# S5 parameter tables beside an MLP: a new order of kp products, masked copies, sums, weight casts and low parts

## The chip, the cores and the metric

The kernel runs on one NeuronCore of one Trainium2 chip. The metric is the device time of one execution in microseconds (us). Engines: PE (TensorE, matrix products), DVE (VectorE), ACT (ScalarE), POOL (GpSimd), and SP, whose queue issues the DMAs. Each runs its own instructions in order and waits for the others by semaphores.

## The reference

One inference step of a two-layer decoder, for 512 prompt tokens and 32 sample tokens (8 sequences of 4), with the same weights. Layer 0 mixes tokens by gated linear attention, layer 1 by an S5 state-space layer; an MLP with squared ReLU follows each:

```python
def _rmsnorm(x, g): ...
for i in range(DEPTH):                       # DEPTH = 2, D_MODEL = 1024, D_FF = 4096
    h = _rmsnorm(x, prm['g_pre_mix'][i])
    m = _gla_mixer(h, ...) if i % 2 == 0 else _s5_mixer(h, ...)
    x = x + _rmsnorm(m, prm['g_post_mix'][i])
    h = _rmsnorm(x, prm['g_pre_mlp'][i])
    f = jnp.square(jax.nn.relu(h @ prm['w_up'][i])) @ prm['w_down'][i]
    x = x + _rmsnorm(f, prm['g_post_mlp'][i])
```

The S5 layer has 64 groups of 64 complex states. Its parameters need much preparation that depends on no token: the step `dt`, the eigenvalues `lam = exp(a * dt)`, `z = (lam - 1) / a`, `bb = z * b`, and products with `c`. The kernel turns the recurrence into products with tables, which it computes from these.

## The kernel before, in words

Activations lie transposed in SBUF: `X[128, 8, 544]`, features on partitions, 544 tokens in two halves of 288 and 256 columns. Products run as fp32r in three passes: high parts of weight and input (`wh`, `xh`), and the two cross terms with the low parts (`wl`, `xl`). Weights come as tiles `raw` of 128 x 1024 by DMA; `split_w` makes `wh` by a cast on ACT (line 111) and `wl = raw - wh` on POOL (line 115; at other times partly or wholly on DVE, line 113), in two parts of 128 x 512 each.

A **job** (`job`) is one weight tile times one half: 24 matmuls into one PSUM bank. Its order in code: the weight splits that a planner (`plan`) set for this job number (`split_at`), then the matmuls, then `finish`, which emits the job's evacuation (`evac`), what was deferred to this job (`after`), and one entry of the list `bg`, the background work. An entry of `bg` is called a slot here; its instructions follow the job's evacuation on every engine. A tile of a four-tile block is used by the first half's four jobs and again by the second half's, and a ring of five buffers decides how early the next cast can be.

In the MLP, "up" jobs compute `h @ w_up`: their evacuation is `r = max(ps, 0) * rs` on DVE (line 350), Square and the cast `hh` on ACT (lines 352, 353), then `hl = r - hh` on DVE (line 354). "Down" jobs multiply `hh`, `hl` with `w_down` and add the result into `acc` on DVE (line 362). Up and down alternate in blocks of 16 jobs.

During the first layer's MLP, after its first up block, `s5_prepare` fills `bg`: 21 slots of small setup work, then sixteen **units** u of four slots each, then three more slots. A unit makes the tables of four S5 groups and stores them to DRAM:

- first slot: `unit_w2` (two products `tmp` on POOL, two products `w` on DVE, lines 1008 to 1011), `unit_t` (five angle instructions `tm`, `ta` on DVE, lines 1069 to 1071)
- second: `unit_w3` (two sums `w` on DVE, lines 1016, 1017, and the store `wd<-w`), `unit_t2` (angle reduction on DVE, lines 1077 to 1080, 872), `unit_w(u+1)` (loads `zb`, `bt`)
- third: `unit_q0` (two products `tmp` on POOL, lines 1029, 1030), `unit_s` (sine `cs<-ta` on ACT, line 1085, then the angle of the cosine on DVE, lines 876 to 878)
- fourth: `unit_k(u-1)`: the kp product on PE (line 1052, eight plain fp32 matmuls of `bbd` and `q`), its copy `kk` on ACT (line 1055), two sums on DVE (line 1058), stores `md<-kk`; then `unit_q(u)`: four instructions `q` on DVE (lines 1035 to 1038), the store, four masked copies `bbd` on ACT (line 1044); then `unit_c` (cosine on ACT, line 1089, and the store)

The bank of kp is called `kp` or `held` in the profile. Of the sixteen units' slots 32 stand behind up jobs, eight at each of the four positions.

Of the kernel before, what the change touches and what calls it, by code (L numbers as in the profile page):

```python
# [12 lines left out]
AF = mybir.ActivationFunctionType  # L13
# [29 lines left out]
def f32(ap):  # L43
    return ap.bitcast(F32)
# [28 lines left out]
class Builder:  # L73
    def __init__(self, tc, io):
        self.tc, self.nc, self.io = tc, tc.nc, io
        self.jobs = 0
        self.after = defaultdict(list)
        self.before_evac = defaultdict(list)
        self.hold, self.held = set(), []
        self.n_tiles = io["w"].shape[0]  # L80
        self.raw, self.wh, self.wl = {}, {}, {}
        self.tile0 = 0
        self.plan()
        self.dve_ks = 1
        self.bg = []
        self.dve_win = None
        self.part = {}
# [5 lines left out]
            self.nc.sync.dma_start(r, self.io["w"][t].rearrange("p (k m) -> p k m", k=KD))  # L93
            self.raw[t] = r

    def split_w(self, t, part=None):

        if part is None:
            self.split_w(t, 0)
            self.split_w(t, 1)  # L100
            return
        nc = self.nc
        r = self.raw[t]
        if part == 0:
            pool = self.p_x if self.in_x[t] else self.p_w
            self.wh[t] = pool.tile([128, KD, 128], F32R, tag="wh", name="wh")
            self.wl[t] = pool.tile([128, KD, 128], F32R, tag="wl", name="wl")
        h, l = self.wh[t], self.wl[t]
        d = self.dve_ks if self.dve_win is None else self.dve_win
        a, b, c = part * 4, part * 4 + d, part * 4 + 4  # L110
        nc.scalar.activation(h[:, a:c], r[:, a:c], AF.Copy)  # L111
        if b > a:
            nc.vector.tensor_sub(l[:, a:b], r[:, a:b], f32(h[:, a:b]))  # L113
        if c > b:
            nc.gpsimd.tensor_sub(l[:, b:c], r[:, b:c], f32(h[:, b:c]))  # L115
        if part:
            del self.raw[t]
            self.load_raw(t + RAW)
# [88 lines left out]

    def finish(self, ps, evac):
        j = self.jobs
        if j in self.hold:  # L210
            self.held.append((ps, evac))
        else:
            for f in self.before_evac.pop(j, []):
                f()
            for p, e in self.held:
                e(p)
            self.held.clear()
            evac(ps)
        for f in self.after.pop(j, []):
            f()  # L220
        if self.bg:
            for f in self.bg.pop(0):
                f()
        self.jobs += 1

    def defer(self, n, f):
# [114 lines left out]
    def mlp(self, g_post, g_next, sink=None, after_first=None, before_last=None):  # L341
        nc = self.nc
        hh = self.p_p.tile([128, KD, NT], F32R, tag="Hh", name="hh")
        hl = self.p_p.tile([128, KD, NT], F32R, tag="Hl", name="hl")

        def up(m, hf, ps):
            c0, c1 = HALF[hf]
            n = c1 - c0
            r = self.p_t.tile([128, 288], F32, tag="r", name="r", bufs=3)
            nc.vector.scalar_tensor_tensor(r[:, :n], ps, 0.0, self.rs[hf][:, :n], op0=OP.max, op1=OP.mult)  # L350
            h = hh[:, m, c0:c1]
            nc.scalar.activation(r[:, :n], r[:, :n], AF.Square)  # L352
            nc.scalar.activation(h, r[:, :n], AF.Copy)
            self.defer(0, lambda: nc.vector.tensor_sub(hl[:, m, c0:c1], r[:, :n], f32(h)))  # L354

        def down(b, m, hf, ps):
            c0, c1 = HALF[hf]
            a = self.acc[:, m, c0:c1]
            if b == 0:
                nc.scalar.activation(a, ps, AF.Copy)  # L360
            else:
                nc.vector.tensor_add(a, ps, a)
            if b == 3:
                self.m_done(m, hf, g_post, g_next, sink)

        for b in range(4):
            for part in ("up", "down"):
                if part == "down" and b == 3 and before_last:
                    before_last()
                sizes = (8,) if PLAN[self.block][0] == 8 else (4, 4)  # L370
                q = 0
                for n in sizes:
                    if part == "up":
                        self.run_block(self.xh, self.xl, lambda i, hf, ps: up(q + i, hf, ps))
                    else:
                        self.run_block(hh, hl, lambda i, hf, ps: down(b, q + i, hf, ps))
                    q += n
                if part == "up" and b == 0 and after_first:
                    after_first()
# [426 lines left out]
    def s5_prepare(self, ctx):  # L806

        nc, io = self.nc, self.io
# [142 lines left out]
        st = {}  # L951
# [50 lines left out]
        def unit_w2(u):  # L1002
            w = p.tile([128, 2, 2, 2, 64], F32, tag="w", name="w")
            zb = st["zb"].rearrange("p r q (g n) -> p r q g n", g=2)
            b = [st["bt"][:, r, :, None, :].to_broadcast([128, 2, 2, 64]) for r in (0, 1)]
            zr, zi = zb[:, 0], zb[:, 1]
            tp = [tmp[:, 256 * i:256 * (i + 1)].rearrange("p (q g n) -> p q g n", q=2, g=2) for i in (0, 1)]
            G.tensor_mul(tp[0], zi, b[1])
            G.tensor_mul(tp[1], zi, b[0])
            V.tensor_mul(w[:, 0], zr, b[0])  # L1010
            V.tensor_mul(w[:, 1], zr, b[1])
            st["w"], st["tp"] = w, tp
# [14 lines left out]
        def unit_q0(u):  # L1027
            l, c, tp = q_parts(u)
            G.tensor_mul(tp[0], l[1], c[1])
            G.tensor_mul(tp[1], l[1], c[0])  # L1030

        def unit_q(u):
            q5 = p.tile([128, 2, 2, 10, 16], F32, tag="q", name="q5")
            l, c, tp = q_parts(u)
            V.tensor_mul(q5[:, 0], l[0], c[0])
            V.tensor_mul(q5[:, 1], l[0], c[1])
            V.tensor_add(q5[:, 0], q5[:, 0], tp[0])
            V.tensor_sub(q5[:, 1], q5[:, 1], tp[1])
            nc.sync.dma_start(self.qd[u].rearrange("p (a b) -> p a b", a=4),
                              q5.rearrange("p r q t c -> p (r q) (t c)")[:, :, 0:128])  # L1040
            bbd = p.tile([128, 2, 2, 2, 16], F32, tag="bbd", name="bbd")
            for r in (0, 1):
                for g in (0, 1):
                    nc.scalar.activation(bbd[:, r, :, g], self.bb[:, r, 2 * u:2 * u + 2], AF.Copy, scale=gm[:, g:g + 1])
            st["q5"], st["bbd"] = q5, bbd

        def unit_k(u):
            ps = self.bank("kp")
            q5, bbd = st["q5"], st["bbd"]
            for q in (0, 1):  # L1050
                for r in (0, 1):
                    nc.tensor.matmul(ps[0:32, q * 128:(q + 1) * 128], bbd[:, r, q].rearrange("p g c -> p (g c)"),
                                     q5[:, r, q, 2:10].rearrange("p t c -> p (t c)"), start=(r == 0), stop=(r == 1))
            kk = self.kk[0]
            nc.scalar.activation(kk[:, :, 0:128], ps[0:32, 0:256].rearrange("p (q n) -> p q n", q=2), AF.Copy)
            for q in (0, 1):
                o = kk[:, q, 96:128]
                V.scalar_tensor_tensor(o, eye, dsk[:, 2 * u + q:2 * u + q + 1], o, op0=OP.mult, op1=OP.add)
                nc.sync.dma_start(self.md[2 * u + q], kk[:, q])
# [4 lines left out]
        def unit_t(u):  # L1064

            a, m = (p.tile([128, 2, 128], F32, tag=n, name=n) for n in ("ta", "tm"))
            col = lambda n, q: t(n)[:, 2 * u + q:2 * u + q + 1]
            for q in (0, 1):
                V.tensor_scalar(m[:, q], iota, col("ptu", q), MAGIC, op0=OP.mult, op1=OP.add)
                V.tensor_scalar(a[:, q], iota, col("phi", q), None, op0=OP.mult)  # L1070
            V.tensor_scalar(m, m, MAGIC, None, op0=OP.subtract)
            st["a"], st["m"] = a, m
# [20 lines left out]
        todo = [load, rest, step_size, magnitude, angles, lams, zs, turn_angle, masks, bbar, z_rows,  # L1093
                *[rest] * 7, z_turn, rest, lambda: unit_w(0)]
        for u in range(16):
            todo += [[lambda u=u: unit_w2(u), lambda u=u: unit_t(u)],
                     [lambda u=u: unit_w3(u), lambda u=u: unit_t2(u)] + ([lambda u=u: unit_w(u + 1)] if u < 15 else []),
                     [lambda u=u: unit_q0(u), lambda u=u: unit_s(u)],
                     ([lambda u=u: unit_k(u - 1)] if u else []) + [lambda u=u: unit_q(u), lambda u=u: unit_c(u)]]
        todo += [rest, rest, lambda: unit_k(15)]  # L1100
        self.bg += [f if isinstance(f, list) else [f] for f in todo]

    def s5(self, ctx):
# [418 lines left out]
```

## Time and profile before

| what | value |
|---|---|
| median of 3 runs | 1404.31 us (1402.98 to 1405.43) |
| the profiled execution's own time | 1405.15 us |
| its span, first to last instruction | 1403.4 us |
| mean granted TensorE clock | 0.968 |
| busy: PE, DVE, ACT, POOL | 94%, 62%, 40%, 46% of the span |

Profile rows give the start in us from the span's start, the duration in us, the engine, the source line, the operation, `out<-in` by the program's names, shapes and a count; in brackets stands the idle time of the engine just before and what ended it. Rows of waits give: who waited, at which line, for which engine and line, then the sum in us, how many times, the longest. Busy times of PE come from modelled ends of pipelined matmuls. A merged row (count over 1) gives the time from the first start to the last end.

### The profile page before, as it was taken

The page shows a single profiled execution, that of the slowest core. Times are in us where ns is not written, and L with a number is a line of the kernel's source. Part 1 is how long each engine was busy: PE and PEld are TensorE (multiplying, and loading weights), DVE is VectorE, ACT ScalarE, POOL GpSimd, SP SyncE. Part 2 cuts the span into 40 slices and gives each one's busy share as a digit, 9 for nine tenths or more (in the row PEclk, how much of TensorE's full clock was granted, in tenths as well). Part 3 has the DMA queues.
Part 4 walks back from the last instruction along what each step waited for, and adds up shares of the span by engine and source line. Part 5 has one row for each costly group of instructions (what it writes and reads, how often), then busy time and mean ns, then how long its engine had stood idle before and what let it go on. Part 6 is the DMA issues. An engine that isn't in the chain of part 4 may idle for free. (4 is left out here: it accounts for less than half of the span.)

```text
span 1403.4 us, 25744 instructions
## 1 busy us (share of the span) xinstructions
PE 1312.2 (94%) x9968; PEld 1278.3 (91%) x9968; DVE 874.9 (62%) x1793; ACT 563.5 (40%) x1283; POOL 639.5 (46%) x715
## 2 busy tenths in 40 slices
PE   7999999989999898889898997899899999999996
PEld 6999999979999797789897997899799999999996
DVE  7865655597437997799648789655871342332345
ACT  6534354645333423323443332344452432432432
POOL 4443344565474674466445343443643333333240
PEclk9999999999999899999999999999999999999998
DMA  5233222312333454445332768432223232323221
GB/s 184 95 120 124 76 95 64 121 61 77 109 109 113 134 162 132 130 141 175 117 106 72 239 183 254 132 99 91 85 66 91 73 109 69 98 76 106 76 61 64
DMA packets 79274, 157.53 MB, mean 112 GB/s; under 512 B 8144, under 2 KB 41808, under 8 KB 78128
## 3 DMA queue, kind: packets, MB, share of 16 engines
q1 hardware_dynamic: 79152, 155.89, 35.6%
q8 instruction: 78, 1.28, 0.4%
q14 instruction: 44, 0.36, 0.1%
HBM read 130.27 MB, written 25.59 MB: 111 GB/s over the span
## 5 line engine op out<-in xcount | busy, mean ns | idle before, releaser
L115 POOL TENSOR_TENSOR wl<-raw,wh 128x384 fp32r<-128x384 f32 (+2 forms) x351 | 422.4, 1217 | 483.9 <-ACT wh L111 482.1
L111 ACT ACTIVATE wh<-raw 128x512 fp32r<-128x512 f32 x368 | 216.3, 618 | 86.5 <-PE held L186 53.4
L186 PE MATMUL held<-xh,wh 128*128 128x288 f32 (+1 forms) x784 | 233.0, 297 | 2.9 <-ACT wh L111 2.8
L186 PE MATMUL held<-xh,wl 128*128 128x288 f32 (+1 forms) x784 | 229.7, 293 | 3.8 <-POOL wl L115 3.8
L186 PE MATMUL held<-xl,wh 128*128 128x288 f32 (+1 forms) x784 | 230.1, 294 | 0.8 <-DVE xl L279 0.8
L186 PE MATMUL mm<-xh,wh 128*128 128x256 f32 (+1 forms) x752 | 221.8, 295 | 0.8 <-ACT wh L111 0.8
L186 PE MATMUL mm<-xl,wh 128*128 128x256 f32 (+1 forms) x752 | 220.1, 293 | 2.1 <-DVE xl L279 2.0
L186 PE MATMUL mm<-xh,wl 128*128 128x256 f32 (+1 forms) x752 | 218.5, 290 | 0.9 <-POOL wl L115 0.9
L113 DVE TENSOR_TENSOR wl<-raw,wh 128x128 fp32r<-128x128 f32 (+2 forms) x247 | 138.2, 568 | 105.6 <-ACT wh L111 100.2
L186 PEld LDWEIGHTS held<-xh,wl 128*128 128x128 f32 x784 | 150.3, 192 | 5.1 <-POOL wl L115 5.1
L186 PEld LDWEIGHTS held<-xh,wh 128*128 128x128 f32 x784 | 150.8, 192 | 4.6 <-ACT wh L111 3.0
L186 PE MATMUL held<-hh,wh 128*128 128x288 f32 (+1 forms) x512 | 150.4, 294 | 4.0 <-ACT wh L111 4.0
L186 PE MATMUL held<-hh,wl 128*128 128x288 f32 (+1 forms) x512 | 150.2, 293 | 3.1 <-POOL wl L115 3.1
L186 PEld LDWEIGHTS held<-xl,wh 128*128 128x128 f32 x784 | 150.7, 192 | 1.4 <-DVE xl L279 1.0
L352 ACT ACTIVATE r<-r 128x256 f32<-128x256 f32 (+1 forms) x128 | 55.1, 431 | 238.3 <-DVE r L350 238.3
L186 PE MATMUL mm<-hh,wh 128*128 128x256 f32 (+1 forms) x512 | 148.8, 291 | 1.7 <-ACT wh L111 1.7
L186 PE MATMUL held<-hl,wh 128*128 128x288 f32 (+1 forms) x512 | 150.0, 293 | 0.0
L186 PE MATMUL mm<-hh,wl 128*128 128x256 f32 (+1 forms) x512 | 148.2, 290 | 1.8 <-POOL wl L115 1.8
L186 PE MATMUL mm<-hl,wh 128*128 128x256 f32 (+1 forms) x512 | 148.8, 291 | 0.0
L186 PEld LDWEIGHTS mm<-xl,wh 128*128 128x128 f32 x752 | 144.8, 193 | 3.4 <-DVE xl L279 3.2
L186 PEld LDWEIGHTS mm<-xh,wh 128*128 128x128 f32 x752 | 145.1, 193 | 2.7 <-issue 1.2
L186 PEld LDWEIGHTS mm<-xh,wl 128*128 128x128 f32 x752 | 144.1, 192 | 1.1 <-POOL wl L115 1.1
(400 smaller groups left out, 2876.1 us busy)
## 6 DMA issues: line engine op xcount, KB each, us to landing
raw<-in_w SPq DMA_DIRECT2D x184, 512.0 KB
S<-in_h SPq DMA_DIRECT2D x4, 1024.0 KB
out_gla_s<-S SPq DMA_DIRECT2D x4, 1024.0 KB
zb<-zd SPq DMA_DIRECT2D x16, 256.0 KB
wd<-w SPq DMA_DIRECT2D x16, 256.0 KB
qd<-q SPq DMA_DIRECT2D x16, 256.0 KB
wd<-cs SPq DMA_DIRECT2D x16, 256.0 KB
qt<-qd SPq DMA_DIRECT2D x16, 256.0 KB
```

The costliest lines, as they stand in the source:

```text
L111: nc.scalar.activation(h[:, a:c], r[:, a:c], AF.Copy)
L113: nc.vector.tensor_sub(l[:, a:b], r[:, a:b], f32(h[:, a:b]))
L115: nc.gpsimd.tensor_sub(l[:, b:c], r[:, b:c], f32(h[:, b:c]))
L186: self.nc.tensor.matmul(ps[:, :c1 - c0], a[:, k], b[:, k, c0:c1], start=(k == 0 and i == 0), stop=(k == KD - 1 and i == 2))
L352: nc.scalar.activation(r[:, :n], r[:, :n], AF.Square)
```

## The change

Nothing is added to the computation or taken from it; the instructions are the same, in another order.

- `finish` emits the casts `wh` of the next job's splits ahead of this job's evacuation while `bg` is not empty. The subtractions stay where they were.
- `hl` of an up job goes to a list `late`, emitted behind the slot's background work. Where there is no such work its place is the old one.
- The masked copies `bbd` of unit u move to the first slot of unit u+1 (`unit_b`), kp to its second slot (`unit_k`), the copy `kk` to the third (`unit_k1`), the sums and stores to the fourth (`unit_k2`). Before, `bbd` stood in the fourth slot of unit u and the other three together in the fourth of unit u+1. The list is one slot longer.

```diff
 def split_w(self, t, part=None, cast_only=False):
...
-        nc.scalar.activation(h[:, a:c], r[:, a:c], AF.Copy)
+        if (t, part) not in self.is_cast:
+            nc.scalar.activation(h[:, a:c], r[:, a:c], AF.Copy)
+        if cast_only:
+            self.is_cast.add((t, part))
+            return
...
 def finish(self, ps, evac):
         j = self.jobs
+        if self.bg:
+            for u in self.split_at.get(self.wjob, []):
+                self.split_w(*u, cast_only=True)
...
         if self.bg:
             for f in self.bg.pop(0):
                 f()
+        for f in self.late:
+            f()
+        self.late.clear()
...
-            self.defer(0, lambda: nc.vector.tensor_sub(hl[:, m, c0:c1], r[:, :n], f32(h)))
+            self.late.append(lambda: nc.vector.tensor_sub(hl[:, m, c0:c1], r[:, :n], f32(h)))
...
+        def unit_b(u):
             bbd = p.tile([128, 2, 2, 2, 16], F32, tag="bbd", name="bbd")
...
+        def unit_k1(u):
+            nc.scalar.activation(self.kk[0][:, :, 0:128], st["kp"][0:32, 0:256].rearrange("p (q n) -> p q n", q=2), AF.Copy)
+
+        def unit_k2(u):
             kk = self.kk[0]
-            nc.scalar.activation(kk[:, :, 0:128], ps[0:32, 0:256].rearrange("p (q n) -> p q n", q=2), AF.Copy)
...
         for u in range(16):
-            todo += [[lambda u=u: unit_w2(u), lambda u=u: unit_t(u)],
-                     [lambda u=u: unit_w3(u), lambda u=u: unit_t2(u)] + ([lambda u=u: unit_w(u + 1)] if u < 15 else []),
-                     [lambda u=u: unit_q0(u), lambda u=u: unit_s(u)],
-                     ([lambda u=u: unit_k(u - 1)] if u else []) + [lambda u=u: unit_q(u), lambda u=u: unit_c(u)]]
-        todo += [rest, rest, lambda: unit_k(15)]
+            todo += [[lambda u=u: unit_w2(u), lambda u=u: unit_t(u)] + ([lambda u=u: unit_b(u - 1)] if u else []),
+                     [lambda u=u: unit_w3(u), lambda u=u: unit_t2(u)] + ([lambda u=u: unit_w(u + 1)] if u < 15 else []) +
+                     ([lambda u=u: unit_k(u - 1)] if u else []),
+                     [lambda u=u: unit_q0(u), lambda u=u: unit_s(u)] + ([lambda u=u: unit_k1(u - 1)] if u else []),
+                     ([lambda u=u: unit_k2(u - 1)] if u else []) + [lambda u=u: unit_q(u), lambda u=u: unit_c(u)]]
+        todo += [[lambda: unit_b(15)], lambda: unit_k(15), lambda: unit_k1(15), lambda: unit_k2(15)]
```

The new lines shift the numbers: `r` is line 361, `hl` 365, `q` 1046 to 1049, `bbd` 1058, kp 1066, `kk` 1071, the sums 1077, the sine 1104, L876 to L878 become 887 to 889.

The first place is DVE, the second slot of unit 1, in an up block. Before:

```order
L350 SCALAR_TENSOR_TENSOR r<-mm,rs_84 128x288
L354 TENSOR_TENSOR hl<-r,hh 128x288
L1016 TENSOR_TENSOR w<-w,tmp 128x256
L1017 TENSOR_TENSOR w<-w,tmp 128x256
L1077 SCALAR_TENSOR_TENSOR ta<-tm,ta 128x256
L1078 SCALAR_TENSOR_TENSOR ta<-tm,ta 128x256
L1080 SCALAR_TENSOR_TENSOR ta<-iota,sm,ta 128x128 x2
L872 TENSOR_SCALAR ta<-ta 128x256
```

The same place on DVE after the change:

```order
L361 SCALAR_TENSOR_TENSOR r<-mm,rs_84 128x288
L1027 TENSOR_TENSOR w<-w,tmp 128x256
L1028 TENSOR_TENSOR w<-w,tmp 128x256
L1096 SCALAR_TENSOR_TENSOR ta<-tm,ta 128x256
L1097 SCALAR_TENSOR_TENSOR ta<-tm,ta 128x256
L1099 SCALAR_TENSOR_TENSOR ta<-iota,sm,ta 128x128 x2
L883 TENSOR_SCALAR ta<-ta 128x256
L365 TENSOR_TENSOR hl<-r,hh 128x288
```

`hl` moved from directly behind `r` to the end of the slot.

The second place is ACT, the fourth slot of unit 15 and the slot behind it (`r` is here the Square, `cs` the cosine). Before:

```order
L352 ACTIVATE r<-r 128x256
L353 ACTIVATE hh<-r 128x256
L1055 ACTIVATE kk_4000<-held 32x2x128
L1044 ACTIVATE bbd<-bb,gm 128x2x16 x4
L1089 ACTIVATE cs<-ta 128x256
L111 ACTIVATE wh<-raw 128x512
L352 ACTIVATE r<-r 128x256
L353 ACTIVATE hh<-r 128x256
L111 ACTIVATE wh<-raw 128x512 x2
```

The same place on ACT after the change:

```order
L113 ACTIVATE wh<-raw 128x512
L363 ACTIVATE r<-r 128x256
L364 ACTIVATE hh<-r 128x256
L1108 ACTIVATE cs<-ta 128x256
L113 ACTIVATE wh<-raw 128x512 x2
L363 ACTIVATE r<-r 128x256
L364 ACTIVATE hh<-r 128x256
L1058 ACTIVATE bbd<-bb,gm 128x2x16 x4
L113 ACTIVATE wh<-raw 128x512 x2
```

Each cast moved ahead of the Square it stood behind, `kk` left the slot, and `bbd` stands behind the `hh` of the next job.

The third place is PE, the last kp product (`mm` and `held` are the two kinds of PSUM banks). Before:

```order
L186 MATMUL mm<-xl,wh 128x256
L186 MATMUL mm<-xh,wl 128x256
L1052 MATMUL held<-q_7671,bbd 32x128 x4
L186 MATMUL mm<-xh,wh 128x288
L186 MATMUL mm<-xl,wh 128x288
```

The same product on PE after the change:

```order
L191 MATMUL held<-xl,wh 128x256
L191 MATMUL held<-xh,wl 128x256
L1066 MATMUL kp<-q_7673,bbd 32x128 x4
L191 MATMUL held<-xh,wh 128x256
L191 MATMUL held<-xl,wh 128x256
```

This kp moved ahead of one more 256-column job; the other fifteen moved ahead of two jobs each.

More of the change, by code (lines that the diff above doesn't have):

```diff
@@ L81, in __init__ @@
         self.raw, self.wh, self.wl = {}, {}, {}
+        self.is_cast, self.late = set(), []
         self.tile0 = 0
@@ L94, in load_raw, with split_w @@
             self.raw[t] = r
-    def split_w(self, t, part=None):
+    def split_w(self, t, part=None, cast_only=False):
         if part is None:
@@ L103, in split_w @@
         r = self.raw[t]
-        if part == 0:
+        if part == 0 and (t, 0) not in self.is_cast:
             pool = self.p_x if self.in_x[t] else self.p_w
@@ L1040, in unit_q @@
                               q5.rearrange("p r q t c -> p (r q) (t c)")[:, :, 0:128])
+            st["q5"] = q5
+        def unit_b(u):
             bbd = p.tile([128, 2, 2, 2, 16], F32, tag="bbd", name="bbd")
@@ L1044, in unit_q @@
                     nc.scalar.activation(bbd[:, r, :, g], self.bb[:, r, 2 * u:2 * u + 2], AF.Copy, scale=gm[:, g:g + 1])
-            st["q5"], st["bbd"] = q5, bbd
+            st["bbd"] = bbd
         def unit_k(u):
@@ L1053, in unit_k @@
                                      q5[:, r, q, 2:10].rearrange("p t c -> p (t c)"), start=(r == 0), stop=(r == 1))
+            st["kp"] = ps
+        def unit_k1(u):
+            nc.scalar.activation(self.kk[0][:, :, 0:128], st["kp"][0:32, 0:256].rearrange("p (q n) -> p q n", q=2), AF.Copy)
+        def unit_k2(u):
             kk = self.kk[0]
-            nc.scalar.activation(kk[:, :, 0:128], ps[0:32, 0:256].rearrange("p (q n) -> p q n", q=2), AF.Copy)
             for q in (0, 1):
```

## The prediction

> **What bounds the kernel now.** I read the page first, for the share of TensorE (PE), then the windows, to find the stretch where PE loses time, then the waits of that stretch, and last the timeline row by row. The stretch is the 64 slots in which the sixteen S5 units run. A quiet stretch of 32 jobs in the second MLP stands beside it.
>
> ```profile
> PE 1312.2 (94%) x9968; PEld 1278.3 (91%) x9968; DVE 874.9 (62%) x1793; ACT 563.5 (40%) x1283; POOL 639.5 (46%) x715
> ```
> ```profile
> 1050.00:1146.80 96.80, 96.80 (x770) 96.80 (x769) 28.25 (x66) 37.32 (x82) 33.13 (x31) 1.00 0.26 80
> 422.70:682.60 259.90, 230.48 (x1689) 219.20 (x1688) 226.25 (x462) 87.83 (x236) 147.83 (x127) 0.95 0.44 139
> ```
>
> The columns after the length are the busy times of PE, PEld, DVE, ACT and POOL, then granted clock, DMA share, GB/s. The first row gives 96.80/32 = 3.025 us a job with PE never idle. The second holds 64 jobs and 16 kp products; at 3.025 and 1.06 (below) that is 210.6 us of PE work in 259.9, so 49 us are lost here, most of what PE loses after the start. VectorE (DVE) is busy 226.2, and the waits say where its other 34 went:
>
> ```profile
> DVE hl L354 <- ACT hh L353: 30.7, 32, 1.0
> PE kp L1052 <- DVE q L1037: 5.4, 3, 2.8
> PE held L1052 <- DVE q L1037: 5.1, 1, 5.1
> ```
>
> DVE waits only for `hh`: 30.7 us in 32 waits, 0.96 each. With them it is full: 226.2 + 30.7 = 256.9 of 259.9. So DVE is the bound of the stretch. PE's waits for kp operands, and for weights whose casts sit in ACT's queue behind an evacuation that waits for DVE, are only how that bound reaches PE. The last wait tells it: at 682.32 PE has stood still for 5.05 us for unit 15's `q`, and from there it runs on. What moves that moment moves the end.
>
> **The change, part by part.**
>
> *hl after the tables.* A slot's `hl` now stands behind the slot's own table work. One slot on a second position of a unit ("first" to "fourth" are a unit's slots):
>
> ```profile
> 446.74 0.45 DVE L350 SCALAR_TENSOR_TENSOR r<-mm,rs 128x288 f32<-128x288 f32 x1
> 447.70 0.44 ACT L353 ACTIVATE hh<-r 128x288 fp32r<-128x288 f32 x1
> 448.17 0.46 DVE L354 TENSOR_TENSOR hl<-r,hh 128x288 fp32r<-128x288 f32 x1 [0.99 <-ACT hh L353]
> 448.55 0.42 DVE L1016 TENSOR_TENSOR w<-w,tmp 128x256 f32<-128x256 f32 x1
> ```
>
> `r` ends at 447.19 and DVE stands until 448.17. After the change L1016 follows `r` at once and `hh` is long done when `hl` comes. Up slots with unit work number 32, eight at each position. First, second and fourth positions gain. The third doesn't:
>
> ```profile
> 451.75 0.45 DVE L350 SCALAR_TENSOR_TENSOR r<-held,rs 128x288 f32<-128x288 f32 x1
> 453.07 0.40 ACT L1085 ACTIVATE cs<-ta 128x256 f32<-128x256 f32 x1
> 453.96 0.43 DVE L877 TENSOR_TENSOR ta<-ta,tm 128x256 f32<-128x256 f32 x1
> 454.63 0.42 DVE L350 SCALAR_TENSOR_TENSOR r<-mm,rs 128x256 f32<-128x256 f32 x1
> ```
>
> There L877 overwrites the `ta` that the sine at 453.07 reads, and the sine stands behind Square and `hh` on ACT; it ends at 453.47. So L877 starts near 453.5 instead of 453.96, L878 follows, and `hl` (0.38 from its start to the next row) fills the rest: the next `r` comes at about 454.55 instead of 454.63. I take nothing. Of the other 24 slots one lies before the first row of the chain (422.72, below), so 23 x 0.96 = 22.1 us leave DVE's chain.
>
> *What comes back as blocking.* Instructions of DVE whose operands lie in SBUF stretch when GpSimd (POOL) runs beside them, and in part of those waits POOL was running undisturbed:
>
> ```profile
> 483.24 0.41 DVE L1017 TENSOR_TENSOR w<-w,tmp 128x256 f32<-128x256 f32 x1
> 597.71 1.50 DVE L1017 TENSOR_TENSOR w<-w,tmp 128x256 f32<-128x256 f32 x1
> 597.59 2.76 POOL L115 TENSOR_TENSOR wl<-raw,wh 128x512 fp32r<-128x512 f32 x2 [2.70 <-ACT wh L111]
> 442.73 0.80 DVE L354 TENSOR_TENSOR hl<-r,hh 128x288 fp32r<-128x288 f32 x1 [0.99 <-ACT hh L353]
> 441.03 1.49 POOL L115 TENSOR_TENSOR wl<-raw,wh 128x512 fp32r<-128x512 f32 x1 [3.23 <-ACT wh L111]
> 666.97 0.81 DVE L354 TENSOR_TENSOR hl<-r,hh 128x288 fp32r<-128x288 f32 x1 [0.99 <-ACT hh L353]
> 665.22 1.55 POOL L115 TENSOR_TENSOR wl<-raw,wh 128x512 fp32r<-128x512 f32 x1 [2.21 <-ACT wh L111]
> ```
>
> The same L1017 takes 0.41 alone and 1.50 beside a `wl`. Laying POOL's rows over the 23 waits, nine have POOL running (first and last shown), 8.25 us in all. How much of a POOL instruction a full DVE pays is seen in two units of a down block, where DVE has no waits at all:
>
> ```profile
> 478.10 1.13 DVE L1010 TENSOR_TENSOR w<-zb,bt 128x256 f32<-128x256 f32 x1
> 490.12 1.17 DVE L1010 TENSOR_TENSOR w<-zb,bt 128x256 f32<-128x256 f32 x1
> 506.08 1.14 DVE L1010 TENSOR_TENSOR w<-zb,bt 128x256 f32<-128x256 f32 x1
> 480.67 1.26 POOL L115 TENSOR_TENSOR wl<-raw,wh 128x512 fp32r<-128x512 f32 x1
> 492.73 5.00 POOL L115 TENSOR_TENSOR wl<-raw,wh 128x512 fp32r<-128x512 f32 x4
> ```
>
> The units last 12.02 and 15.96; the second meets about four more `wl`, 0.99 us each for 1.25 of POOL time, or 79%. 0.79 x 8.25 = 6.5 us come back; ends 0 and 8.25. The chain gets 22.1 - 6.5 = 15.6 us shorter. The Trainium skill (SBUF — State Buffer, section "SBUF: two separate sides") calls the port pair of VectorE and GpSimd an exclusive lock held for the whole instruction. By that rule all 8.25 us return and the sum below would be 1.75 us worse; the stretched L1017 agrees with the lock, the 79% says that some of POOL's time still falls beside rows that don't need it.
>
> *Casts ahead of evacuations.* The casts themselves (0.62 us each) are the same ones. They need no `r`, only PE's last read of the old tile and the raw load, so `wh` and `wl` come about a slot earlier. POOL's order does not change and SP's differs by one raw load that passes two `md` stores at the very end. While PE is ahead of DVE the cast hides in the evacuation's wait for `r`. Value: nothing by itself, since DVE is the bound; it takes the weight waits away, which then reappear at kp.
>
> *kp earlier on PE, masked copies later on ACT.* kp of unit u stood behind the job of the next unit's fourth slot; now behind the second slot, while its `bbd` comes from that unit's first slot. PE may be only about two jobs ahead instead of four. This costs something at two places. First at the end:
>
> ```profile
> 422.72 0.96 DVE L1010 TENSOR_TENSOR w<-zb,bt 128x256 f32<-128x256 f32 x1
> 680.36 0.94 ACT L1044 ACTIVATE bbd<-bb,gm 128x32 f32<-128x32 f32 x4
> 682.10 0.47 DVE L1038 TENSOR_TENSOR q<-q,tmp 128x320 f32<-128x320 f32 x1
> 682.32 1.88 PE L1052 MATMUL held<-q,bbd 128*32 128x128 f32 x8 [5.05 <-DVE q L1037]
> 682.50 0.41 DVE L350 SCALAR_TENSOR_TENSOR r<-mm,rs 128x256 f32<-128x256 f32 x1
> 683.39 0.42 ACT L353 ACTIVATE hh<-r 128x256 fp32r<-128x256 f32 x1
> ```
>
> The chain runs from 422.72 to 682.57. Behind the last `q` now come `hl` (0.35), then `r` to the end of `hh` (682.50 to 683.81, 1.3), then `bbd` (0.94) before kp may start: about 2.8 us later than its 682.32, against `q`. And one job more (a 256-column one, 2.85) remains behind it. Together 5.6 us. The ends are 2.85, if the copies are ready in time and only the job counts, and 7, if that job runs as slowly as the one at 459.89 below (4.04). Second, PE and DVE are now tied by a loop: `r` of a first slot, `hh` (1.4), `bbd` (0.94), kp, and three jobs until DVE's next first `r`. With kp at 1.06 and 3 x 3.025 that is 12.5 us. After a wait PE runs slower:
>
> ```profile
> 442.22 1.06 PE L1052 MATMUL held<-q,bbd 128*32 128x128 f32 x8
> 458.07 1.89 PE L1052 MATMUL kp<-q,bbd 128*32 128x128 f32 x8 [2.84 <-DVE q L1037]
> 459.89 0.61 PE L186 MATMUL held<-hh,wh 128*128 128x288 f32 x1
> 463.93 0.29 PE L186 MATMUL mm<-hh,wh 128*128 128x288 f32 x1
> 536.63 0.94 DVE L1010 TENSOR_TENSOR w<-zb,bt 128x256 f32<-128x256 f32 x1
> 553.52 0.95 DVE L1010 TENSOR_TENSOR w<-zb,bt 128x256 f32<-128x256 f32 x1
> 574.48 0.96 DVE L1010 TENSOR_TENSOR w<-zb,bt 128x256 f32<-128x256 f32 x1
> ```
>
> kp takes 0.83 more, and the 288-column job behind it 4.04 (459.89 to 463.93) where such a job takes 3.20 in the chain of the quiet stretch (3.025 is the mean with the 256-column ones): 0.84 more.
>
> ```profile
> 1053.45 3.20 PE mm L186 x24
> ```
>
> The slow loop is 14.2 us. Units of up blocks take DVE 16.89 and 20.96 now; less three waits, 14.0 and 18.1 before any blocking comes back. So DVE stays the longer side, but in every second unit barely; I take 1 us in all for DVE starved of jobs (ends 0 and 6: eight units, 0.75 each). The Trainium skill (TensorE: Matmul & The Clock Gate, section "What's actually happening") has the clock halve after an idle window of about 3.4 us. By that, waits under 3.4 us cost nothing more, and the sum would be 1 us better; the kp of 1.89 us after a wait of 2.84 speaks against leaning on it.
>
> *Sums and evacuation of kp.* The copy of kp moves one slot ahead of the sums, both with the same instructions; they hide behind ACT's idle time (87.8 us busy of 259.9) and a sum that no longer waits for its copy. Nothing. Outside the slots with S5 work the order is the old one.
>
> **Sum.** 22.1 - 6.5 - 5.6 - 1.0 = 9.0 us less. The profiled execution took 1405.15 us for a span of 1403.4; it would be 1396.1. That execution lies 0.84 above the median of the runs, 1404.31, so against the median 1395.3; I say 1395. With all ends good 22.1 - 2.85 = 19.2 less, 1385; with all ends bad 22.1 - 8.25 - 7 - 6 = 0.9 less, 1403.
>
> **Rivals.**
> - *Slower: the short lead ties PE and DVE.* If the loop, not DVE, sets each unit's pace, every kp wait makes PE slow, the slow kp and job (1.68 us) starve DVE, and so on. At 1.68 for all sixteen units, 26.9 us in place of my 1.0: 1404.3 - 10.0 + 26.9 = 1421; at half of it 1408. It decides from 10.0/16 = 0.63 us a unit on. For it: 14.2 against 14.0. Against it: the other up units have 4 us to spare, and in down blocks kp waits for `q` alone (the copies need no `r` there), so that the loop is 1.4 shorter.
> - *No change that can be told.* The waits are gone but POOL's 8.25 us and the end's 7 come back in full, with 5 us of starving: 1402. Measured runs of this kernel spread by about 0.2%, 2.8 us, which is what can be told from no change.
> - *Much faster.* With `wl` spread over more slots POOL meets DVE's evacuations from PSUM, which show no stretching, more often, and four stretches like that of L1017 (1.1 us each) fall away instead of new ones coming: 22.1 + 4.4 - 5.6 = 20.9 less, 1383. Against it: POOL's order is unchanged and DVE leaves fewer gaps.
>
> **How the numbers follow.** Forecast 0.66 (own range 1387 to 1402), slower by the loop 0.13, no change 0.11, much faster 0.10. Faster than 1401.5: the forecast nearly whole and the last rival, 0.75; within 0.2%: 0.13; slower than 1407.1: 0.12. The range leaves out half of the last rival and the larger part of the first: 1384 to 1406.
>
> **What would show it.** In the changed profile the wait of `hl` for `hh` should fall from 32 cases to nearly none, with L888 (the old L877) waiting for the sine at about eight third positions. DVE should be busy in nearly all of the stretch, which should last about 245 us from the first L1021 to the last `q` instead of 259.85, and its contended rows should have a few us more. PE's waits for `wh` and `wl` should shrink, those of kp grow, naming ACT's `bbd`. The last kp should start near 670.5 (682.32 - 15.6 + 2.8 + 1.0). Wrong would be: DVE idle before `r` for PE in the stretch (the loop), or a stretch as long as before with longer DVE rows (blocking).

## The result and the profile after

| | median of 4 runs | profiled span | granted clock |
|---|---|---|---|
| before | 1403.64 us (1402.09 to 1405.43) | 1403.4 us | 0.968 |
| after | 1391.21 us (1390.16 to 1392.86) | 1389.8 us | 0.970 |

The ratio is 0.9912, 95% interval 0.9895 to 0.9929: 12.4 us less, 10.0 to 14.7. The forecast was 1395. (Below, a gain in us is always one minus the ratio times the median of before beside it; the ratio can differ from the quotient of the two medians by up to 0.2%.)

From the page of the changed kernel, the line of busy times, and from its windows the stretch from the first `w` product to the last `q` (columns as in the prediction):

```profile
PE 1305.9 (94%) x9968; PEld 1274.3 (92%) x9968; DVE 876.2 (63%) x1793; ACT 566.1 (41%) x1283; POOL 638.0 (46%) x715
418.94:664.39 245.45, 221.85 (x1648) 212.91 (x1648) 229.22 (x461) 89.86 (x234) 146.69 (x128) 0.94 0.46 147
```

The page hardly moves: PE's busy time falls by 6 us. The stretch tells more: 245.45 us where it was 259.85. DVE is 3.0 us busier there (229.22 against 226.20) and still stands still for 16.2. The waits of that stretch say for what, and where PE now loses its time:

```profile
PEld held L1066 <- ACT bbd L1058: 21.8, 10, 6.5
DVE ta L888 <- ACT cs L1104: 8.5, 8, 1.1
PE held L1066 <- DVE q L1048: 6.0, 4, 2.0
DVE r L361 <- PE mm L191: 4.6, 7, 1.6
```

No row has `hl` waiting for `hh` any more, nor PE for `wh` or `wl`. In place of 30.7 us DVE waits 8.5 us for the sine, in eight third positions, and 4.6 us for PE before `r`. PE's waits stand at kp, for ACT's copies or for `q`.

The end, in the timeline: the last `q` of DVE, the last copies, the last kp, and the jobs behind it (the first rows of three jobs).

```profile
663.92 0.47 DVE L1049 TENSOR_TENSOR q<-q,tmp 128x320 f32<-128x320 f32 x1
666.14 0.94 ACT L1058 ACTIVATE bbd<-bb,gm 128x32 f32<-128x32 f32 x4
667.65 1.06 PE L1066 MATMUL kp<-q,bbd 128*32 128x128 f32 x8
668.64 0.39 PE L191 MATMUL held<-xh,wh 128*128 128x256 f32 x1
671.60 0.30 PE L191 MATMUL mm<-xh,wh 128*128 128x288 f32 x1
674.79 0.29 PE L191 MATMUL held<-xh,wh 128*128 128x288 f32 x1
```

And of before, the job behind its last kp and the next one:

```profile
684.13 0.61 PE L186 MATMUL mm<-xh,wh 128*128 128x288 f32 x1
688.59 0.29 PE L186 MATMUL held<-xh,wh 128*128 128x288 f32 x1
```

The jobs at 674.79 and 688.59 are the same one, the second of four 288-column jobs. I use its start as the mark at which PE is past everything that the change touches. Before it came 6.02 us after the last `q` (688.59 - 682.57), after 10.40 us (674.79 - 664.39). So the stretch gave 14.40 and the end took back 4.38: 10.0 us.

**Stretch plus end, for every kernel below.** Each row comes from one profiled execution: the window of its stretch, its waits, and the start of the marked job. "Sum" is the change of stretch and end against before (259.85 + 6.02). "Measured" is from the ratio, with its interval. Of DVE's waits, "sine" stands for those of the cosine's argument for ACT and "PE" for those of `r` and `acc`. Sum and measured time agree to 2.7 us or better in every row, so no more than that is left for the rest of the program to explain. The time before the stretch is left out of the sum: it lies between 415.20 and 422.72 us, and two kernels that differ only in the last unit (after, and after with the last kp back) came to the stretch at 418.94 and 421.58.

| kernel | stretch | DVE busy | DVE waits: hh / sine / copy of kp / PE | end | sum | measured |
|---|---|---|---|---|---|---|
| before | 259.85 | 226.20 | 30.7 / 0 / 0 / 0 | 6.02 | | |
| after | 245.45 | 229.22 | 0 / 8.5 / 0 / 4.6 | 10.40 | -10.0 | -12.4 (-14.7 to -10.0) |
| after, again | 243.38 | 229.01 | 0 / 8.6 / 0 / 2.7 | 10.40 | -12.1 | -10.4 (-12.9 to -8.0) |
| hl alone | 251.53 | 231.38 | 0 / 8.5 / 8.5 / 1.1 | 5.71 | -8.6 | -8.3 (-10.2 to -6.2) |
| kp alone | 260.45 | 226.81 | 30.7 / 0 / 0 / 0 | 10.57 | +5.2 | +2.5 (+0.1 to +4.9) |
| casts alone | 261.10 | 227.47 | 30.7 / 0 / 0 / 0 | 5.45 | +0.7 | +1.0 (-1.0 to +2.9) |
| hl and casts | 251.72 | 231.55 | 0 / 8.5 / 8.5 / 0 | 6.72 | -7.4 | -9.4 (-11.5 to -7.3) |
| late kp, split sums | 244.82 | 233.11 | 0 / 8.5 / 0 / 0.7 | 5.87 | -15.2 | -15.4 (-17.9 to -12.9) |
| the same, early sine | 236.50 | 232.13 | 0 / 0.5 / 0 / 0 | 6.48 | -22.9 | -21.9 (-24.8 to -18.9) |
| after, early sine | 238.66 | 229.96 | 0 / 0 / 0 / 5.4 | 10.41 | -16.8 | -18.9 (-22.0 to -15.7) |
| after, last kp back | 242.39 | 228.55 | 0 / 8.6 / 0 / 2.8 | 10.40 | -13.1 | -13.0 (-15.6 to -10.7) |
| after, last two back | 244.76 | 229.85 | 0 / 8.6 / 0 / 3.9 | 4.58 | -16.5 | -17.8 (-20.5 to -15.0) |
| early sine, phase on ACT | 230.11 | 225.63 | 0 / 0 / 0 / 0 | 4.18 | -31.6 | -31.7 (-35.1 to -28.5) |
| early sine, wl twice | 265.16 | 260.86 | 0 / 0.5 / 0 / 0.7 | 5.72 | +5.0 | +4.1 (+1.8 to +6.2) |

### The profile page after: what moved, and what is told of

Read it like the earlier page. It is cut to its first block, busy times and chain, and to the rows that moved or that the text cites. A ratio compares the mean times of both kernels' runs of the same rounds, so it can differ in the third digit from the quotient of the medians.

```text
span 1389.8 us, 25728 instructions
## 1 busy us (share of the span) xinstructions
PE 1305.9 (94%) x9968; PEld 1274.3 (92%) x9968; DVE 876.2 (63%) x1793; ACT 566.1 (41%) x1283; POOL 638.0 (46%) x715
## 5 line engine op out<-in xcount | busy, mean ns | idle before, releaser
L191 PE MATMUL held<-xh,wh 128*128 128x256 f32 (+1 forms) x792 | 233.6, 295 | 0.1
L191 PE MATMUL held<-xl,wh 128*128 128x256 f32 (+1 forms) x792 | 230.8, 291 | 0.8 <-DVE xl L290 0.8
L191 PE MATMUL held<-xh,wl 128*128 128x256 f32 (+1 forms) x792 | 229.5, 290 | 0.0
L191 PE MATMUL mm<-xh,wh 128*128 128x288 f32 (+1 forms) x744 | 222.7, 299 | 0.0
L191 PE MATMUL mm<-xl,wh 128*128 128x288 f32 (+1 forms) x744 | 220.9, 297 | 1.6 <-DVE xl L290 1.6
L191 PE MATMUL mm<-xh,wl 128*128 128x288 f32 (+1 forms) x744 | 219.2, 295 | 0.0
L191 PE MATMUL mm<-hh,wh 128*128 128x288 f32 (+1 forms) x512 | 148.5, 290 | 0.0
L191 PE MATMUL mm<-hl,wh 128*128 128x288 f32 (+1 forms) x512 | 148.4, 290 | 0.0
L191 PE MATMUL mm<-hh,wl 128*128 128x288 f32 (+1 forms) x512 | 147.8, 289 | 0.0
L191 PE MATMUL held<-hl,wh 128*128 128x256 f32 (+1 forms) x512 | 147.7, 288 | 0.0
```

Source lines behind the costliest of these rows:

```text
L191: self.nc.tensor.matmul(ps[:, :c1 - c0], a[:, k], b[:, k, c0:c1], start=(k == 0 and i == 0), stop=(k == KD - 1 and i == 2))
```

## The experiments

My theory was the prediction's: DVE bounds the stretch, its waits for `hh` are the gain, and the early kp costs at the end. The rivals were that hl alone gains nothing, since PE is tied to DVE by the weight casts as well; that the casts are the gain; and that the early kp is needed.

### The three parts one by one

In every kernel below with kp at its old place one thing more differs from before: on ACT the cosine (0.40 us) stands ahead of the masked copies, not behind them. So kp can start a little later than before; the order of DVE's instructions is not touched.

**hl alone** (before, with only this):

```diff
-            self.defer(0, lambda: nc.vector.tensor_sub(hl[:, m, c0:c1], r[:, :n], f32(h)))
+            self.late.append(lambda: nc.vector.tensor_sub(hl[:, m, c0:c1], r[:, :n], f32(h)))
```

> Only hl stands behind the table work; kp products, copies, sums and weight casts are where they were before the change. Theory (DVE is the bound of the S5 stretch, and its waits for hh are all that the change wins): the stretch from the first w product to the last q is 13 to 17 us shorter than the 259.85 of before (23 waits of 0.96 less what comes back as blocking), and since kp of the last unit needs no copies behind q here, the end price of 4.4 us that the changed kernel pays is not paid: 13 to 17 us off the whole time, 1387 to 1391, some 3 us below the changed kernel. Rival (hl alone does nothing, since the weight casts behind the evacuations tie PE to DVE as hard as the waits for hh did): PE's waits for wh and wl grow, DVE waits for PE before r, and the time falls by less than 6 us, 1398 or more.

Measured: ratio 0.9941 (0.9927 to 0.9956), 8.3 us less. Neither expectation fits: the stretch is 8.3 us shorter, not 13 to 17, but PE's waits for the weights don't tie DVE (it waits 1.1 us for PE). The waits of the stretch name what I had not thought of, and the timeline shows one:

```profile
DVE kk L1074 <- ACT kk L1068: 8.5, 7, 1.3
DVE ta L885 <- ACT cs L1101: 8.5, 8, 1.1
450.56 0.42 DVE L358 SCALAR_TENSOR_TENSOR r<-mm,rs 128x256 f32<-128x256 f32 x1
452.17 0.40 DVE L1074 SCALAR_TENSOR_TENSOR kk<-cst,dsk,kk 32x32 f32<-32x32 f32 x2 [1.20 <-ACT kk L1068]
```

In a fourth slot kp's copy stands on ACT behind Square and `hh`, and the sum that needs it comes right after `r`. The wait for `hh` had covered that; when `hl` moves away, the sum waits 1.2 us in its place. So in seven fourth slots the gain depends on another part of the change, the one that puts sums a slot behind their copy.

**kp alone** (the change without `late` and without casts ahead of evacuations):

> Only the kp products, their masked copies and sums are moved as in the change; hl follows its evacuation and the casts follow theirs, as before. Theory: the stretch stays near 259.85 us, DVE waits for hh in 32 cases of 0.96 as before, and the end is 4 to 6 us longer (the copies behind the last q, and one job more behind the last kp): 1407 to 1409. Rival (the move is free, or helps by itself because kp no longer stands in front of two jobs): 1401 to 1405.

Measured: 1.0018 (1.0001 to 1.0035), 2.5 us more. The trace has what was expected: the stretch 260.45, `hl` waiting for `hh` 30.7 us, and an end of 10.57 us, 4.55 more than before. The times alone don't decide: the median of 1404.26 lies in the rival's range, before beside it took 1401.76, and the ratio's interval takes in 4 us and zero only just not. At this end PE is in time and the copies are late, as the prediction had it (the second row is PE's weight load for kp):

```profile
683.98 0.94 ACT L1055 ACTIVATE bbd<-bb,gm 128x32 f32<-128x32 f32 x4
684.55 0.14 PEld L1063 LDWEIGHTS kp<-q,bbd 128*32 128x32 f32 x2 [2.28 <-ACT bbd L1055]
```

The last `q` had ended at 682.84.

**Casts alone** (the change without `late` and with the old kp order):

```diff
+        if self.bg:
+            for u in self.split_at.get(self.wjob, []):
+                self.split_w(*u, cast_only=True)
```

> Only the weight casts precede the evacuations; hl and kp are as before. Theory: PE's waits for wh and wl in the stretch (some 20 us before) go to the kp products, DVE stays full with its waits for hh, the stretch is within 2 us of 259.85 and the time within 1.5 us of before. Rival (the casts are what frees PE and so wins the time): 6 us or more below before, 1398 or less.

Measured: 1.0007 (0.9993 to 1.0021). PE's wait before the last kp is 6.99 us where it was 5.05, and all its waits at kp are 23.7 us where they were 10.5. Its waits for `wh` before the jobs are gone (9.4 us before), those for `wl` are not (9.1 us against 9.5), so only part of what was expected went to kp; DVE did not notice. The casts by themselves show no gain, as predicted.

**hl and casts**, with the old kp order:

> The changed kernel with the kp products, copies and sums put back to their old places: hl after the tables and casts ahead of the evacuations. Theory: DVE's chain is as in the changed kernel or up to 4 us shorter (the longer lead of PE takes away the 4.7 us in which DVE waits for PE), and the end price of 4.4 us goes: 4 to 8 us below the changed kernel, 1383 to 1387. Rival (the early kp is needed, since a kp that waits for q holds the job of the next unit's fourth slot): 1391 or more.

Measured: 0.9933 (0.9918 to 0.9948), 9.4 us less. The theory fell, and for the reason that the first run gave: the stretch is 251.72 with the same 8.5 us of sums waiting for copies. The median of 1391.90 is in the rival's range, but not for its reason, as the next kernel shows. The end is near its old length, 6.72.

### Late kp with split sums, and the early sine

If that reading is right, the old place of kp with the new split of copy and sums should take both gains. **Late kp, split sums**, cut to its core:

```diff
-            todo += [[..., unit_b(u - 1)], [..., unit_k(u - 1)], [..., unit_k1(u - 1)], [unit_k2(u - 1), unit_q(u), unit_c(u)]]
+            todo += [[..., unit_k1(u - 2)], [..., unit_k2(u - 2)], [...], [unit_k(u - 1), unit_q(u), unit_c(u), unit_b(u)]]
```

> The changed kernel, but the copies stand behind q in the fourth slot and kp behind the job of the next unit's fourth slot, as before the change; the copy of kp and the sums stay split, one slot each, and so come three slots later than in the changed kernel. Theory (the parts of the changed kernel are worth: 30.7 us of waits for hh gone, 8.5 us of waits for the sine new, some 4.6 us of DVE waiting for PE from the short lead, 4.4 us at the end; and a sum that stands in the slot of its own copy costs another 8.5 us, as the two kernels with the old kp order show): here the sums don't wait, PE leads by four jobs and the end is as before, so the stretch is 240 to 244 us and the time 15 to 18 us under before, 4 to 6 us under the changed kernel. Rival (the bank that kp holds a slot longer, or more blocking by POOL, eats it): stretch 247 or more, time 12 us or less under before.

Measured: 0.989 (0.9872 to 0.9908), 15.4 us less. The theory holds in its total and in the end (5.87); the stretch is at 244.82, just over its 244:

```profile
415.60:660.42 244.82, 222.64 (x1701) 212.20 (x1699) 233.11 (x460) 88.14 (x236) 141.82 (x128) 0.99 0.45 147
```

DVE waits 0.7 us for PE, not 4.6, but it is busy 233.11 us, 3.9 more than in the changed kernel. It is not that POOL had room in the waits for PE: laid over DVE's standstills of more than 0.15 us, POOL's rows run in them for 8.25 us before the change, 0.5 in the changed kernel (1.6 when run again) and not at all here. But POOL is 4.9 us less busy here (141.82 against 146.69). So in the changed kernel POOL's own instructions got longer where here DVE's did; what decides which of the two pays is not shown.

**The same, early sine:**

```diff
+            for f in self.bg[0]:
+                if isinstance(f, tuple):
+                    f[0]()
...
-                     [lambda u=u: unit_q0(u), lambda u=u: unit_s(u)],
+                     [(lambda u=u: unit_s(u),), lambda u=u: unit_q0(u), lambda u=u: unit_s1(u)],
```

(The first lines stand in `finish`, behind the casts and ahead of the evacuation. `unit_s` is now only the sine on ACT, `unit_s1` the argument of the cosine on DVE.)

> As the kernel with late kp and split sums, and in third slots the sine is issued on ACT ahead of the up job's evacuation, right behind the casts. Theory (DVE is still the bound; the sine waits for nothing but the end of its own argument): the 8 waits of 1.05 us before the cosine's argument fall to under 0.3 us each, one to two us come back as blocking, the stretch is 6 to 7 us shorter than without it (234 to 237 us) and the time 21 to 24 us under before. Rival (PE now starves DVE, or POOL's blocking takes the place of the waits): 3 us or less gained over the same kernel without the early sine.

Measured: 0.9844 (0.9823 to 0.9865), 21.9 us less, as expected: the stretch is 236.50, 8.3 shorter where 6 to 7 were expected, and only 0.5 us of DVE's waits is left. No blocking came back (DVE is busy 232.13 us against 233.11).

**After, early sine** (the same edit on the changed kernel):

> The changed kernel with only the sine moved ahead of the evacuation. Theory (the short lead of kp is what keeps PE from feeding a faster DVE: the loop of r, hh, copies, kp and three jobs): the sine's 8.5 us go, but DVE's waits for PE before r grow from 4.6 to 7 us or more, and the gain over the changed kernel is 2 to 5 us, less than the same edit gives where kp is late. Rival (the lead does not matter): the full 6 to 8 us, as with late kp.

Measured: 0.9865 (0.9843 to 0.9888), 18.9 us less, which is 6.5 to 8.5 better than the changed kernel's two ratios. That is the rival's number. But the stretch got only 4.7 to 6.8 us shorter (238.66 against 243.38 and 245.45) where the same edit gave 8.3 with late kp, and DVE waits 5.4 us for PE where it waited 2.7 to 4.6. The short lead costs something, 1.5 to 3.6 us; the times alone don't show it.

### The end

**After, last kp back.** Only unit 15's copies and kp stand where they were before the change (the copies behind the cosine; kp's own copy and sums follow in slots of their own):

> The changed kernel with only the last unit's copies and kp back at their old places (copies behind its q, kp one job later); its copy and sums follow in slots of their own. Theory (the end price is real): the time from the last q to the job of slot 88's start falls from 10.4 us to about 6 and the time is 4 us under the changed kernel, 15 us under before. Rival (the end price is hidden or is given back because PE then stands still for q and runs slowly after): within 1.5 us of the changed kernel.

Measured: 0.9907 (0.9889 to 0.9924), 13.0 us less, within the first of the changed kernel's intervals and at the edge of the second (0.9908 to 0.9943, below). The end is what decides, and it did not move: 10.40 us from the last `q` (663.97) to the marked job, though kp now stands one job later. PE's rows of that end:

```profile
652.60 1.91 PE L1066 MATMUL held<-q,bbd 128*32 128x128 f32 x8 [3.38 <-ACT bbd L1058]
670.08 1.06 PE L1066 MATMUL held<-q,bbd 128*32 128x128 f32 x8
671.07 0.40 PE L191 MATMUL mm<-xh,wh 128*128 128x288 f32 x1
674.37 0.29 PE L191 MATMUL held<-xh,wh 128*128 128x288 f32 x1
```

The last kp waits for nothing: its `q` had ended 6 us earlier. PE has been at work since 652.60, where unit 14's early kp had waited for its copies. PE is what is late.

**After, last two back.** Units 14 and 15 get the late order (copies, kp and sums), the other fourteen keep the early one:

```diff
+        late = (14, 15)
...
+            e = [u - 1] if u and u - 1 not in late else []
+            o = [u - 1] if u and u - 1 in late else []
```

> The changed kernel with copies, kp and sums of the last two units (14 and 15) at the places of the kernel with late kp. Theory (putting back the last unit alone left 10.4 us from the last q to the second job behind its kp, because PE had run without a wait since the early kp of unit 14 at 652 and was itself late; it is PE's place in the loop, not the copies behind the last q, that makes the end longer): with both back, PE reaches the last kp early and waits for it, those 10.4 us fall to about 6, and the time is 3 to 5 us under the changed kernel run beside it. Rival (the end does not depend on the kp of unit 14): 10 us or more stay, and the time is within 1.5 us of the changed kernel.

Measured: 0.9873 (0.9854 to 0.9893), 17.8 us less. The end fell to 4.58:

```profile
652.12 1.06 PE L1066 MATMUL held<-q,bbd 128*32 128x128 f32 x8
661.87 1.16 PE L1066 MATMUL held<-q,bbd 128*32 128x128 f32 x8
662.96 0.40 PE L191 MATMUL mm<-xh,wh 128*128 128x288 f32 x1
666.25 0.29 PE L191 MATMUL held<-xh,wh 128*128 128x288 f32 x1
```

Unit 14's kp no longer waits, PE comes to the last kp 0.20 us after its `q` (661.67), no wait is shown, and kp (1.16 us) and the job behind it (3.29) run at nearly full speed. That beats the 6.02 of before, where PE stood for 5.05 us and ran the next job in 4.46. The theory's place is right; it had foreseen that PE waits there, and it doesn't.

**The changed kernel again**, beside these:

> The changed kernel itself, once more beside the others. Expected 11 to 14 us under before; stretch 242 to 246 us, of which DVE is busy 228 to 230 and waits 8.5 us for the sine and 2 to 5 us for PE before r.

Measured: 0.9926 (0.9908 to 0.9943), 10.4 us less. That is just under the 11 to 14 expected; the stretch and DVE's waits are as expected. The intervals of the two measurements of the changed kernel overlap, and the sum of either trace lies in them or at their edge. The kernel with the last two back is 7.4 us under it from the two ratios, and 4.4 from the two sums, where 3 to 5 were expected.

### What bounds the stretch, and POOL's price

**Early sine, phase on ACT.** If DVE is the bound, work taken off it shortens the stretch:

```diff
-                V.tensor_scalar(a[:, q], iota, col("phi", q), None, op0=OP.mult)
+                nc.scalar.activation(a[:, q], iota, AF.Copy, scale=t("phi")[:, 2 * u + q:2 * u + q + 1])
```

(the new line stands at the start of the unit's first slot, ahead of the evacuation)

> As the kernel with late kp and early sine, and the product of iota and phi (two instructions a unit, 32 in all, 22.5 us of DVE's busy time there with blocking, 0.28 each without) is made by ACT at the start of the unit's first slot. Theory (DVE is still the bound, and POOL's time is paid by whatever SBUF instruction of DVE comes next): DVE's busy time falls by the unblocked 6 to 10 us only, the stretch from 236.5 to 226 to 231 us, and the time is 28 to 33 us under before. Rivals: the whole 22.5 us fall away with their blocking, and PE, with 210.6 us of work, becomes the bound (stretch 213 to 220, over 37 us under before); or ACT makes it late and DVE waits for it (gain under 3 us).

Measured: 0.9774 (0.975 to 0.9797), 31.7 us less, the fastest of all. The windows of the kernel with early sine, and of this one:

```profile
418.30:654.80 236.50, 221.12 (x1702) 210.78 (x1700) 232.13 (x459) 89.87 (x238) 141.75 (x128) 1.00 0.46 152
415.35:645.46 230.11, 219.41 (x1702) 210.94 (x1700) 225.63 (x427) 99.15 (x271) 142.76 (x128) 1.00 0.49 156
```

DVE's busy time fell by 6.5 us and the stretch by 6.4, though the removed group had shown 22.5 us. Its rows, in the kernel with early sine, tell the difference:

```profile
L1093 DVE TENSOR_SCALAR ta<-iota,sm 128x128 f32<-128x128 f32 x32 | 22.5, 703 | 0.0
537.54 5.40 POOL L120 TENSOR_TENSOR wl<-raw,wh 128x512 fp32r<-128x512 f32 x4
540.45 1.32 DVE L1093 TENSOR_SCALAR ta<-iota,sm 128x128 f32<-128x128 f32 x1
542.94 0.28 DVE L1093 TENSOR_SCALAR ta<-iota,sm 128x128 f32<-128x128 f32 x1
```

0.28 is the instruction when no `wl` runs (0.20 to the next row's start, or 6.4 us for 32). The rest came from POOL's `wl`, beside which it took 1.32; since DVE's busy time fell by 6.5 and not 22.5, that rest went to other DVE instructions. A stretched group's busy time is not what its removal is worth.

**Early sine, wl twice** measures that price by itself:

```diff
             nc.gpsimd.tensor_sub(l[:, b:c], r[:, b:c], f32(h[:, b:c]))
+            if part == 0 and 5 < len(self.bg) <= 69:
+                nc.gpsimd.tensor_sub(l[:, b:c], r[:, b:c], f32(h[:, b:c]))
```

> As the kernel with late kp and early sine, but POOL makes the first half of each weight's low part twice in the stretch (32 more instructions of 1.36 us, 44 us of POOL). Theory (a full DVE pays 79% of POOL's time, the price that the prediction took from two units of before): DVE is 30 to 40 us busier, the stretch grows from 236.5 to 267 to 277 us, and the time is 8 to 18 us over before. Rival (POOL's extra time falls into what does not meet DVE, or only instructions that are already stretched pay): the stretch grows by less than 18 us and the time stays under before.

Measured: 1.0029 (1.0013 to 1.0044), 4.1 us over before. Its window, and its group of the added instructions:

```profile
415.20:680.36 265.16, 226.97 (x1703) 212.41 (x1702) 260.86 (x460) 90.03 (x238) 184.16 (x160) 0.99 0.42 136
L122 POOL TENSOR_TENSOR wl<-raw,wh 128x512 fp32r<-128x512 f32 x32 | 43.6, 1362 | 2.5
```

POOL is 42.4 us busier (184.16 - 141.75), DVE 28.7 (260.86 - 232.13), the stretch 28.7 longer. A full DVE pays 68% of POOL's time, not 79%; the sizes measured lie just under the ranges expected, and the rival is out. The Trainium skill (SBUF — State Buffer, section "SBUF: two separate sides") has the shared port pair held for the whole instruction. That DVE pays at all agrees. Of the 13.7 us that DVE did not pay half is seen: beside `r` and `acc`, which read PSUM and take at most 0.46 us in every kernel here, POOL runs 15.4 us where it ran 8.6. Where the other half went is not shown.

## Why the prediction was right, and where its steps were not

- **The bound: right, shown.** DVE fills the stretch in every kernel here, and its length is DVE's busy time, its listed waits and 2 to 5 us of short gaps. Work taken off DVE shortens it one for one (6.5 and 6.4), time put on through POOL lengthens it one for one (28.7 and 28.7).
- **22.1 us of waits: the size right, the cause half right.** DVE's waits for ACT fell from 30.7 to 8.5 us, 22.2, and the eight third positions that gain nothing are there. But the prediction gave this to the move of `hl`, and priced "sums and evacuation of kp" at nothing. With `hl` and casts alone 8.5 us come back at the sums; splitting them from their copy is worth 6.9 us of stretch (251.72 against 244.82). The step that failed is the one that asked what was late next: it asked so for the sine, and for the sum only with the split already in place.
- **6.5 us of blocking: measured 3.0**, and 2.8 when run again. The amount was nearly right: of the 8.25 us that POOL ran undisturbed 0.5 are left (1.6 again). The price was not: of what came back in the changed kernel DVE paid 39% and 42%, where the forecast had 79%. In hl alone, in hl and casts and in the two kernels with late kp, reckoned the same way, it paid 72 to 84%. Early kp goes with the lower price and with a POOL that is itself busy longer; the reason stays open.
- **1.0 us of DVE starved by PE: measured 4.6 and 2.7**, inside its ends 0 and 6. With the blocking it makes 7.6 and 5.5 where 7.5 was forecast. The first agrees because two errors cancel, which is luck.
- **5.6 us at the end: 4.4, by another mechanism.** The prediction made it of the last unit's late copies (2.8) and of one job more (2.85). With both undone the end was as long, 10.40. PE itself is late, from unit 14's early kp on, and both causes end within a microsecond of each other: in the changed kernel the copies end at 667.08 and PE comes at 667.65. With both units back the 4.4 us are gone, and 1.4 more. The prediction's own mechanism is seen with kp alone, where PE is in time and waits for the copies.
- **Casts at nothing: right** as far as the times can tell (-1.0 to +2.9 us by themselves), and in the changed kernel PE waits at kp and no longer for weights. By themselves the casts took away only the waits for `wh`.
- **The signs.** `hl` waits for `hh` nowhere in the stretch, L888 waits for the sine in eight, the stretch is 245.45 against "about 245", PE's waits name `bbd`. The last kp started at 667.65 against 670.5; this execution came to the first product 3.78 us earlier (418.94 against 422.72), and counted from there it is 0.9 us late.
- **The sum.** Forecast 9.0, by the traces 10.0 and 12.1, by the times 12.4 and 10.4. The rival of the slow loop is real but small: 0.2 to 0.3 us a unit, where 0.63 would have decided. The other two rivals, 1402 and 1383, lie outside the measured interval.

Still open: why two executions of the changed kernel differ by 2 us of DVE waiting for PE. The waits of the runs name PE and kp, and nothing here tells what sets their phase.

## What to carry to other kernels

When a wait is taken out of a full engine's queue, look at everything that stood behind it in the same slot and ask for each what it needs from the engine that was waited for: here eight arguments of a cosine had been hidden by the wait and took its place, and seven sums would have, had they stayed in the slot of their copy. Move a product ahead in an in-order queue only as far as its operands are early. For the last units it did not pay here at all: nothing gave back what PE lost there. And do not price an instruction by a busy time that another engine stretches; only its short form goes away with it.

## Of the hardware, not expected

Waits of PE of the same length cost different amounts, and short ones can cost as much as long ones. Before the change the kp after 2.84 us of waiting took 1.89 us and the job behind it was slow. In the kernel with phase on ACT one waited 2.87 us, and both ran at nearly full speed. In the changed kernel run again, 3.42 us of waiting left a kp of 1.30 us and then a job that began with 0.61 us matmuls and took 4.75:

```profile
645.20 1.22 PE L1070 MATMUL held<-q,bbd 128*32 128x128 f32 x8 [2.87 <-DVE q L1052]
646.35 0.40 PE L191 MATMUL mm<-xh,wh 128*128 128x288 f32 x1
649.64 0.29 PE L191 MATMUL held<-xh,wh 128*128 128x288 f32 x1
```
```profile
651.39 1.30 PE L1066 MATMUL held<-q,bbd 128*32 128x128 f32 x8 [3.42 <-ACT bbd L1058]
652.63 0.61 PE L191 MATMUL mm<-xh,wh 128*128 128x288 f32 x1
657.38 0.28 PE L191 MATMUL held<-xh,wh 128*128 128x256 f32 x1
```

With hl and casts a wait of only 1.48 us left a kp of 1.86 us, at a granted clock of 0.61 (the second row is the window over it, with the clock third from its end):

```profile
471.39 1.86 PE L1066 MATMUL held<-q,bbd 128*32 128x128 f32 x8 [1.48 <-DVE q L1048]
471.30:473.20 1.90, 1.79 (x9) 1.05 (x9) 1.90 (x4) 0.00 (x0) 1.88 (x3) 0.61 0.18 53
```

The Trainium skill (TensorE: Matmul & The Clock Gate, section "What's actually happening") has the clock follow a window that runs free of the program, which fits a slow spell that begins at kp in one case and inside it in another. Its window of about 3.4 us as the least idle time does not agree with the kp of 1.89 us after 2.84, nor with that of 1.86 after 1.48.
